# Two-layer decoder trunk: block norm's sum by two float32r products, stacked gate weights, 640 keys in two halves, sooner split of transposed probabilities in layer 1

## The chip, the cores and the metric

One core of a Trainium2 chip runs the whole program. The metric is the time of one execution in device microseconds (us); with one core, the slowest core is that core. TensorE (PE) multiplies, VectorE (DVE) and ScalarE (ACT) work on what it leaves in PSUM, GpSimd (POOL) helps, and SyncE (SP) issues most transfers. Each engine works its own list of instructions in order; semaphores tie the lists together.

## What is computed

Two decoder layers over 1024 positions of width 1024, in float32. Layer 0 uses differential attention (8 heads with two score maps each), layer 1 forgetting attention (16 heads with a learned decay). Each is followed by a residual with layer norm, a gated MLP of width 2816 with a causal convolution, and another layer norm. Cut to what the change touches:

```python
# layer 0, per block of 128 queries
s = einsum('bhcqd,bhckd->bhcqk', qb, k) * scale
p = masked_softmax(s, causal_mask(start, Q_BLOCK, S))
a = p[:, :, 0] - lam * p[:, :, 1]
o = einsum('bhqk,bhkd->bqhd', a, v)
o = rms_norm(o, subln_g) * (1.0 - lambda_init)   # mean of squares over the 128 of a head
# layer 1
q, k, v, f_logit = split(x @ w_in, ...)          # f_logit: 16 columns
log_f = log_sigmoid(f_logit + b_f); c = cumsum(log_f, axis=1)
s = einsum('bhqd,bhkd->bhqk', qb, k) * scale + cb[..., :, None] - c[..., None, :]
o = einsum('bhqk,bhkd->bqhd', masked_softmax(s, mask), v)
```

## The kernel before

**Number form.** A float32 operand x is split into a high part (x rounded to float32r, by an ACT copy, L89) and a low part (the rest, by a DVE subtraction, L91 or L93). A product of two split operands is three float32r products, high by high, high by low and low by high: `mm3`, L100 to L102. The low by low product is left out everywhere. Where one operand is a transposed probability of layer 1, two products do (L1397 and L1398).

**Attention by pairs.** `attention(l)` goes over 8 pairs of 64-wide head parts. During a pair its scores, softmax and value products run, and in between the projections of the next pair (`project`, 48 steps) are fed to PE as filler; in the last pair the filler is the output projection. A job is one block of 128 queries of one score map. Its parts are spread over ticks: `scores` (L533, L534), the mask and row minimum on DVE (`top`, L540) with the first tick; the exponential on ACT (L578, layer 1 L694) and the division on DVE (L581 to L588, layer 1 L697 and L698) later. A block of query number qt has (qt+1) x 128 keys, and `scores` takes them in chunks of up to 512 columns, so 640 keys are a chunk of 512 and one of 128. Each chunk has two products.

**Values.** When the blocks of a group (four query blocks; in the last pair of layer 0 also two groups of two) are done, a `Values` object turns their probabilities with PE transposes (`turn_one`, L1371) into a PSUM tile "m", splits them (`evacuate`, tiles "pt" from the pool probT with three buffers) and multiplies them with the values (`products`). One round of the main loop is `tick` (next job's scores, products of what is split, `evacuate`, exponentials, divisions), some projection steps, and `tock` (`turn`, `finish`), with the remaining steps behind. So transposes of one tock are split in the next tick and multiplied in the one after. The pool for "m" has four banks, shared by projections, transposes, values and sums.

**Block norm.** In layer 0, `diff_values` ends a group: ACT copies the values to "of" (L600) and squares them (L602); one float32 product with a 128 x 128 tile of ones (L606) sums over the head; ACT takes the logarithm and the exponential (L608, L609), and four DVE operations (L610 to L613) apply the result.

**Gate logits.** At the start of layer 1, `gate_logits(c)` multiplies the 16 gate columns with the 8 blocks of x, three products each, for the two halves c of the positions; DVE adds the bias (L636). The first call stands at the seam of layer 0's MLP and layer 1, the second inside `first_pair`.

**What sets the order.** The Python code gives a program order; a scheduler then orders the instructions of every engine by its own picture of what is ready, and the buffer pools decide the waits. So an edit in one place can move instructions elsewhere. Weights come by transfer into "wst" tiles (two buffers, used in layer 0 for probabilities too) and are cut into "wh" and "wl" by ACT and DVE.

## Time and profile before

| quantity | value |
|---|---|
| median of 3 runs (lowest to highest) | 2470.56 us (2469.18 to 2472.64) |
| profiled execution, its own time | 2472.59 us |
| its span, first to last instruction | 2470.8 us |
| PE busy in the span | 2421.0 us, 11377 matmul records |
| DVE, ACT, POOL busy | 1893.9, 1239.2, 141.2 us |
| mean granted clock of TensorE | 0.994 |
| layer 0's attention from 98 to 435 us: PE, DVE, ACT busy | 329.60, 266.99, 189.76 us of 337 |
| layer 1's attention from 1280 to 1740 us: PE, DVE, ACT busy | 456.96, 354.50, 257.83 us of 460 |

A row of the timeline has the start in us from the span's start, the duration in us, engine, line, operation, output and inputs by the program's names (buffer numbers left out), the shape, the count, and in brackets the idle time before it and what ended it. PE records overlap: the next matmul starts before the last one's listed end. A row of the windows has the stretch, its length, then busy time and count for PE, PEld (weight loads), DVE, ACT and POOL, the granted clock, the share of the DMA engines and GB/s.

### The profile page before, as it was taken

The page shows a single profiled execution, that of the slowest core. Times are in us where ns is not written, and L with a number is a line of the kernel's source. Part 1 is how long each engine was busy: PE and PEld are TensorE (multiplying, and loading weights), DVE is VectorE, ACT ScalarE, POOL GpSimd, SP SyncE. Part 2 cuts the span into 40 slices and gives each one's busy share as a digit, 9 for nine tenths or more (in the row PEclk, how much of TensorE's full clock was granted, in tenths as well). Part 3 has the DMA queues.
Part 4 walks back from the last instruction along what each step waited for, and adds up shares of the span by engine and source line. Part 5 has one row for each costly group of instructions (what it writes and reads, how often), then busy time and mean ns, then how long its engine had stood idle before and what let it go on. Part 6 is the DMA issues. An engine that isn't in the chain of part 4 may idle for free. (4 is left out here: it accounts for less than half of the span.)

```text
span 2470.8 us, 32550 instructions
## 1 busy us (share of the span) xinstructions
PE 2421.0 (98%) x11377; PEld 1984.9 (80%) x11377; DVE 1893.9 (77%) x3588; ACT 1239.2 (50%) x2311; POOL 141.2 (6%) x323
## 2 busy tenths in 40 slices
PE   9999999999999999989999999999999999999998
PEld 7887778778888888878778888888878888888776
DVE  5887877989767667696857777778888666666978
ACT  4555556556544444434545555555465444445344
POOL 2111111010000000000100000000010000000000
PEclk9999999999999999999999999999999999999999
DMA  6223223532322224842422222224223222228622
GB/s 182 65 84 91 81 82 92 174 110 80 103 77 77 95 85 140 298 157 74 138 70 73 65 65 65 65 81 155 94 79 101 77 89 90 77 85 301 206 86 98
DMA packets 111940, 266.02 MB, mean 108 GB/s; under 512 B 17648, under 2 KB 24816, under 8 KB 111776
## 3 DMA queue, kind: packets, MB, share of 16 engines
q1 hardware_dynamic: 110816, 262.83, 33.4%
q8 instruction: 90, 1.47, 0.2%
q0 software_dynamic: 672, 1.05, 0.2%
q14 instruction: 74, 0.61, 0.1%
q10 hardware_dynamic: 288, 0.07, 0.0%
HBM read 182.68 MB, written 47.64 MB: 93 GB/s over the span
## 5 line engine op out<-in xcount | busy, mean ns | idle before, releaser
L100 PE MATMUL m<-xh,wh 128*128 128x512 f32 x768 | 320.3, 417 | 7.0 <-DVE pt L91 6.6
L101 PE MATMUL m<-xl,wh 128*128 128x512 f32 x768 | 302.7, 394 | 1.7 <-DVE xl L91 1.7
L102 PE MATMUL m<-xh,wl 128*128 128x512 f32 x768 | 302.8, 395 | 0.0
L100 PE MATMUL m<-xh,wo 128*128 128x512 f32 x656 | 255.4, 389 | 0.0
L102 PE MATMUL m<-xh,wo 128*128 128x512 f32 x656 | 255.3, 389 | 0.0
L101 PE MATMUL m<-xl,wo 128*128 128x512 f32 x656 | 255.2, 389 | 0.0
L89 ACT ACTIVATE pt<-m 128x512 fp32r<-128x512 f32 (+3 forms) x285 | 137.6, 492 | 182.8 <-PE m L1371 120.6
L540 DVE CUSTOM_DVE_ANT_0 s<-s,mask 128x384 f32<-128x384 f32 (+7 forms) x256 | 194.5, 760 | 42.4 <-PE s L534 41.5
L89 ACT ACTIVATE wo<-wg 128x512 fp32r<-128x512 f32 x168 | 106.5, 634 | 225.0 <-PE m L102 218.4
L100 PE MATMUL m<-q,wo 128*128 128x512 f32 x472 | 184.1, 390 | 0.0
L91 DVE TENSOR_TENSOR pt<-m,pt 128x512 fp32r<-128x512 f32 (+3 forms) x285 | 156.7, 558 | 35.6 <-ACT pt L89 31.7
L101 PE MATMUL m<-q,wo 128*128 128x512 f32 x472 | 183.8, 389 | 0.0
L102 PE MATMUL m<-q,wo 128*128 128x512 f32 x472 | 183.7, 389 | 0.0
L100 PEld LDWEIGHTS m<-xh,wh 128*128 128x128 f32 x768 | 145.7, 190 | 38.3 <-DVE pt L91 11.2
L102 PEld LDWEIGHTS m<-xh,wl 128*128 128x128 f32 x768 | 145.0, 189 | 31.3 <-DVE wl L91 0.2
L101 PEld LDWEIGHTS m<-xl,wh 128*128 128x128 f32 x768 | 145.5, 190 | 27.5 <-issue 2.9
L89 ACT ACTIVATE wo<-t 128x512 fp32r<-128x512 f32 x132 | 82.8, 627 | 145.3 <-PE m L102 133.2
L91 DVE TENSOR_TENSOR wo<-wg,wo 128x512 fp32r<-128x512 f32 x168 | 115.3, 687 | 41.1 <-ACT wo L89 40.2
L527 POOL CAST qz<-q 64x128 fp32r<-64x128 f32 x256 | 96.6, 378 | 845.1 <-PE s L534 773.2
L100 PEld LDWEIGHTS m<-xh,wo 128*128 128x128 f32 x656 | 123.1, 188 | 26.0 <-ACT pt L1093 0.6
L101 PEld LDWEIGHTS m<-xl,wo 128*128 128x128 f32 x656 | 123.1, 188 | 25.7
L102 PEld LDWEIGHTS m<-xh,wo 128*128 128x128 f32 x656 | 123.1, 188 | 25.6 <-DVE wo L91 0.2
(341 smaller groups left out, 5875.6 us busy)
## 6 DMA issues: line engine op xcount, KB each, us to landing
wst<-in_w SPq DMA_DIRECT2D x46, 512.0 KB, 3.9
t<-in_wi SPq DMA_DIRECT2D x44, 512.0 KB, 4.5
ad<-t SPq DMA_DIRECT2D x44, 512.0 KB, 3.7
ha<-ad SPq DMA_DIRECT2D x88, 256.0 KB, 5.5
wg<-in_wi SPq DMA_DIRECT2D x42, 512.0 KB, 3.5
wb<-in_wd SPq DMA_DIRECT2D x84, 256.0 KB, 3.2
q<-q SPq DMA_DIRECT2D x128, 128.0 KB, 2.2
pt<-in_wd SPq DMA_DIRECT2D x48, 256.0 KB, 4.5
```

The costliest lines, as they stand in the source:

```text
L89: nc.scalar.activation(hi, src, AF.Copy, scale=1.0 if scale is None else scale)
L91: nc.vector.tensor_tensor(lo, src, hi.bitcast(F32), op=ALU.subtract)
L100: mm(out, wh, xh, start=start, stop=False)
L101: mm(out, wh, xl, start=False, stop=False)
L102: mm(out, wl, xh, start=False, stop=stop)
L527: nc.gpsimd.tensor_copy(qz[r:r + 64, :], q[r:r + 64, qt * P:qt * P + P])
L540: self.nc.vector.tensor_tensor_reduce(sb[:, :ln], sb[:, :ln], self.mask[:, 1024 - ln:], 1.0, BIG, ALU.add, ALU.min, mn)
```

## The change

Five edits.

1. *Block norm.* For pairs 0 to 6 the squares are split, and the sum is two float32r products by ones (high and low part). The last pair keeps the float32 product. The reciprocal root goes to a tile of its own ("rd", from the pool bcast; in the last pair a "pt" tile), ACT squares it, and three DVE operations instead of four apply it.
2. *Gate logits.* The high and low parts of the gate weights stand side by side in one tile of 48 columns per block (16 high, 16 zeros, 16 low), taken from the "pt" buffers instead of a tile of its own. One product by the high part of x gives both sums, in rows 0 to 15 and 32 to 47; a second one takes the high weights by the low part of x. DVE adds rows 32 to 47 in an operation of its own. POOL writes the zeros.
3. *640 keys.* Two chunks of 320, set so that they meet at the border of the two PSUM banks.
4. *Layer 1's splits.* `evacuate` runs in `tock`, right behind the transposes, and no longer in the next `tick`. In layer 0 it stays.
5. *The tile of ones* is float32r, read as float32 where it was read as such.

```diff
@@ -134,8 +134,8 @@
             for t in self.qz[h]:
                 nc.gpsimd.memset(t[64 - 64 * h:128 - 64 * h, :].bitcast(F32), 0.0)
         self.nz = [0, 0]
-        self.ones = cp.tile([P, P], F32, name="ones")
-        nc.vector.memset(self.ones, 1.0)
+        self.ones = cp.tile([P, P], F32R, name="ones")
+        nc.vector.memset(self.ones.bitcast(F32), 1.0)
         self.cw, self.cb = [], []
         for l in range(2):
             cw = cp.tile([P, NF, 3], F32, name=f"cw{l}")
@@ -528,8 +528,10 @@
         m = 66 if l else P
         ln = (qt + 1) * P
         sb = self.sbank()
-        for c in range((ln + 511) // 512):
-            ks = slice(c * 512, min(ln, c * 512 + 512))
+        w = ln // 2 if ln == 640 else 512
+        sb = sb[:, 512 - w:512 - w + ln]
+        for c in range(0, ln, w):
+            ks = slice(c, min(ln, c + w))
             nc.tensor.matmul(sb[:, ks], q[:, qt * P:qt * P + P], kd[:, ks], start=True, stop=False)
             nc.tensor.matmul(sb[:, ks], qz[:m], kl[:m, ks], start=False, stop=True)
         return sb, ln
@@ -594,22 +596,32 @@
             self.ofs[p] = self.otile()
         return self.ofs[p]
 
-    def diff_values(self, of, ob, q0, q1):
+    def diff_values(self, of, ob, q0, q1, p):
         nc, w = self.nc, (q1 - q0) * P
         osl = of[:, q0 * P:q1 * P]
         nc.scalar.copy(osl, ob[:, :w])
-        rd = self.tp.tile([P, 512], F32, tag="sq", name=self.nm("sq"), bufs=1)[:, :w]
-        nc.scalar.activation(rd, osl, AF.Square)
+        sq = self.tp.tile([P, 512], F32, tag="sq", name=self.nm("sq"), bufs=1)[:, :w]
+        nc.scalar.activation(sq, osl, AF.Square)
+        last = p == NP - 1
+        if not last:
+            hl = self.lp.tile([P, 1024], F32R, tag="lg", name=self.nm("hl"))
+            h, l = hl[:, :w], hl[:, 512:512 + w]
+            self.split(h, l, sq)
         for _ in range(1 + FL):
             yield
         ms = self.mbank()[:, :w]
-        nc.tensor.matmul(ms, self.ones, rd, start=True, stop=True)
-
+        if last:
+            nc.tensor.matmul(ms, self.ones.bitcast(F32), sq, start=True, stop=True)
+            rd = self.tt.tile([P, 1024], F32, tag="pt", name=self.nm("rd"))[:, :w]
+        else:
+            nc.tensor.matmul(ms, self.ones, h, start=True, stop=False)
+            nc.tensor.matmul(ms, self.ones, l, start=False, stop=True)
+            rd = self.lp.tile([P, 1024], F32, tag="lg", name=self.nm("rd"))[:, :w]
         nc.scalar.activation(rd, ms, AF.Ln, scale=1.0 / P, bias=self.eps_rms)
         nc.scalar.activation(rd, rd, AF.Exp, scale=-0.5)
-        nc.vector.scalar_tensor_tensor(ms, ms, P * RMS_EPS, rd, op0=ALU.add, op1=ALU.mult)
+        nc.scalar.activation(sq, rd, AF.Square)
         nc.vector.scalar_tensor_tensor(osl, osl, self.gsub, rd, op0=ALU.mult, op1=ALU.mult)
-        nc.vector.tensor_tensor(ms, ms, rd, op=ALU.mult)
+        nc.vector.scalar_tensor_tensor(ms, ms, P * RMS_EPS, sq, op0=ALU.add, op1=ALU.mult)
         nc.vector.scalar_tensor_tensor(osl, ms, -3.0 * P, osl, op0=ALU.add, op1=ALU.mult)
 
     def otile(self):
@@ -620,8 +632,9 @@
         if c == 0:
             st = self.tmp()[:, :P]
             nc.sync.dma_start(st, self.i["wf"])
-            self.wf = [self.cp.tile([P, 128], F32R, name=f"wf{j}") for j in range(2)]
-            self.split(*self.wf, st)
+            self.wf = self.tt.tile([P, 1024], F32R, tag="pt", name="wf")[:, :48 * KT].rearrange("p (k n) -> p k n", k=KT)
+            nc.gpsimd.memset(self.wf[:, :, 16:32].bitcast(F32), 0.0)
+            self.split(self.wf[:, :, :16], self.wf[:, :, 32:], st.rearrange("p (k n) -> p k n", k=KT))
             self.bf = self.cp.tile([16, 1], F32, name="bf")
             nc.sync.dma_start(self.bf, self.i["bf"])
             self.z = self.tmp()
@@ -630,10 +643,13 @@
             nc.sync.dma_start(self.tri, self.i["tri"])
         ps = self.mbank()
         for kt in range(KT):
-            ws = slice(16 * kt, 16 * kt + 16)
-            self.mm3(ps[:16], self.wf[0][:, ws], self.wf[1][:, ws], self.xh[kt, c], self.xl[kt, c],
-                     kt == 0, kt == KT - 1)
-        nc.vector.tensor_scalar(self.z[:16, c * 512:c * 512 + 512], ps[:16], self.bf, None, op0=ALU.add)
+            both = self.wf[:, kt], self.xh[kt, c]
+            high = self.wf[:, kt, :16], self.xl[kt, c]
+            for i, (w, x) in enumerate((both, high) if kt == 0 else (high, both)):
+                nc.tensor.matmul(ps[:w.shape[1]], w, x, start=kt + i == 0, stop=kt == KT - 1 and i == 1)
+        z = self.z[:16, c * 512:c * 512 + 512]
+        nc.vector.tensor_scalar(z, ps[:16], self.bf, None, op0=ALU.add)
+        nc.vector.tensor_tensor(z, ps[32:48], z, op=ALU.add)
 
     def forget_gates(self):
 
@@ -655,7 +671,7 @@
             nc.vector.scalar_tensor_tensor(l, l, 1.0 / k, u if k > 1 else e, op0=ALU.add, op1=ALU.mult)
         nc.vector.tensor_scalar(z, z, 0.0, None, op0=ALU.min)
         nc.vector.scalar_tensor_tensor(l, l, -2.0, z, op0=ALU.mult, op1=ALU.add)
-        nc.vector.tensor_tensor_scan(c, self.ones, l, 0.0, op0=ALU.mult, op1=ALU.add)
+        nc.vector.tensor_tensor_scan(c, self.ones.bitcast(F32), l, 0.0, op0=ALU.mult, op1=ALU.add)
         self.c, self.cw8 = c, w
 
     def forget_sums(self):
@@ -784,7 +800,8 @@
         for v in values:
             v.products()
         for v in values:
-            v.evacuate()
+            if v.l == 0:
+                v.evacuate()
         keep = []
         for e in live:
             e[1] += 1
@@ -808,6 +825,9 @@
         n = 1 if values and values[0].l == 0 else 2
         for v in values:
             n -= v.turn(n)
+        for v in values:
+            if v.l:
+                v.evacuate()
         for v in values:
             v.finish()
         return [v for v in values if not v.over]
@@ -1398,7 +1418,7 @@
                     mm(o, self.v[0][:, vs], l, start=False, stop=last)
                 if last:
                     a = k.of_tile(self.p), self.ob, self.q0, self.q1
-                    self.end = k.diff_values(*a) if self.l == 0 else k.fox_values(*a, self.h)
+                    self.end = k.diff_values(*a, self.p) if self.l == 0 else k.fox_values(*a, self.h)
                     self.ob = None
         self.hl = []
 
```

The scheduler then makes another order in many places. Three of them follow, as the built programs have it.

ACT in layer 0, around the border of two pairs, before. L89 is the copy of a split ("pt" transposed probabilities, "q" queries and keys, "wh" a weight cut out of "wst"), L578 an exponential, L608 and L609 the norm, L458 a projection's result:

```order
L89 ACTIVATE pt_2104<-m_2073 128x256
L578 ACTIVATE wst_2110,ls_2059<-s_2052,nm_2057 128x768
L89 ACTIVATE q_1676<-t_1703 128x512
L89 ACTIVATE q_1678<-t_1704 128x512
L89 ACTIVATE wh_2224<-wst_2142 128x1024
L608 ACTIVATE sq_2028<-m_2114,eps_rms 128x512
L89 ACTIVATE pt_2161<-m_2112 128x128
L609 ACTIVATE sq_2028<-sq_2028 128x512
L578 ACTIVATE p_2168,ls_2100<-s_2093,nm_2098 128x896
L458 ACTIVATE t_1704<-m_2039 128x512
L578 ACTIVATE wst_2213,ls_2157<-s_2150,nm_2155 128x896
```

The same place now (L580 the exponential, L620 to L622 the norm with its new Square):

```order
L89 ACTIVATE pt_2122<-m_2091 128x256
L580 ACTIVATE wst_2128,ls_2077<-s_2070,nm_2075 128x768
L89 ACTIVATE q_1689<-t_1718 128x512
L89 ACTIVATE q_1691<-t_1719 128x512
L89 ACTIVATE pt_2181<-m_2130 128x128
L620 ACTIVATE rd_2135<-m_2132,eps_rms 128x512
L580 ACTIVATE p_2188,ls_2118<-s_2111,nm_2116 128x896
L621 ACTIVATE rd_2135<-rd_2135 128x512
L458 ACTIVATE t_1719<-m_2057 128x512
L622 ACTIVATE sq_2043<-rd_2135 128x512
L89 ACTIVATE wh_2247<-wst_2162 128x1024
L580 ACTIVATE wst_2233,ls_2177<-s_2170,nm_2175 128x896
```

The last split of the group, "pt" of 128 columns, stood behind the weight cut "wh" and the first step of the norm; now it stands ahead of both, and so do the norm and two more operations. On DVE the subtraction of that split has moved ahead of "wl" in the same way, at the end of pairs 0 to 5, but not of pair 6.

DVE at the seam to layer 1, behind the first gate call, before. L1476 to L1510 are layer norm, "wl" the low parts of the first two weights of layer 1, L636 the bias of the gate logits:

```order
L1476 TENSOR_SCALAR nm_11097<-sums_9401 128x1
L91 TENSOR_TENSOR wl_11178<-wst_11175,wh_11177 128x1024
L91 TENSOR_TENSOR wl_11184<-wst_11181,wh_11183 128x1024
L1487 TENSOR_SCALAR n_2033_11098<-n_2033_11098 128x1
L1510 SCALAR_TENSOR_TENSOR p_9353<-p_9353,nm_11097,lg_9402 128x768
L1489 SCALAR_TENSOR_TENSOR n_2035_11100<-n_2034_11099,n_2033_11098 128x1
L636 TENSOR_SCALAR t_11136<-m_11140,bf 16x512
```

The same place now (L651 the bias, L652 the added rows 32 to 47):

```order
L1496 TENSOR_SCALAR nm_11170<-sums_9474 128x1
L651 TENSOR_SCALAR t_11209<-m_11213,bf 16x512
L91 TENSOR_TENSOR wl_11244<-wst_11241,wh_11243 128x1024
L1507 TENSOR_SCALAR n_2064_11171<-n_2064_11171 128x1
L1530 SCALAR_TENSOR_TENSOR p_9426<-p_9426,nm_11170,lg_9475 128x768
L1509 SCALAR_TENSOR_TENSOR n_2066_11173<-n_2065_11172,n_2064_11171 128x1
L652 TENSOR_TENSOR t_11209<-m_11213,t_11209 16x512
L1513 SCALAR_TENSOR_TENSOR n_2065_11172<-n_2066_11173,n_2065_11172 128x1
L91 TENSOR_TENSOR wl_11250<-wst_11247,wh_11249 128x1024
```

The bias, which reads the gate's sum, has moved from behind both cuts to ahead of the first.

PE in layer 1, in the middle of a pair, before. L1371 is a transpose into a PSUM tile "m", L1397 and L1398 are the value products by the high and low part of a split "pt"; pt_14136 and pt_14139 are the splits of transposes some 35 rows earlier, and the split of the tile m_14152 transposed here is first multiplied some 30 rows later:

```order
L1371 MATMUL m_14152<-ident,t_14009 128x128
L1371 MATMUL m_14152<-ident,p_14067 128x128
L102 MATMUL m_14077<-xh_11015,wl_13967 128x512
L100 MATMUL m_14077<-xh_11059,wh_13966 128x512
L101 MATMUL m_14077<-xl_11060,wh_13966 128x512
L102 MATMUL m_14077<-xh_11059,wl_13967 128x512
L533 MATMUL s_14172<-q_13380,q_13378 128x512
L534 MATMUL s_14172<-q_13382,qz_281 128x512
L1397 MATMUL m_14178<-pt_14136,q_12723 128x512
L1398 MATMUL m_14178<-pt_14136,q_12723 128x512
L1397 MATMUL m_14178<-pt_14139,q_12723 128x512
L1398 MATMUL m_14178<-pt_14139,q_12723 128x512
```

The corresponding place now (L1391 the transpose, L1417 and L1418 the value products, L535 and L536 the scores); pt_14225 is the split of the tile m_14217 that is transposed here:

```order
L1391 MATMUL m_14217<-ident,p_13971 128x128
L1391 MATMUL m_14217<-ident,p_14015 128x128
L1391 MATMUL m_14217<-ident,t_14072 128x128
L1391 MATMUL m_14217<-ident,p_14130 128x128
L102 MATMUL m_14146<-xh_11132,wl_14037 128x512
L535 MATMUL s_14243<-q_13449,q_13447 128x512
L536 MATMUL s_14243<-q_13451,qz_281 128x512
L1417 MATMUL m_14202<-pt_14222,q_12792 128x512
L1418 MATMUL m_14202<-pt_14222,q_12792 128x512
L1417 MATMUL m_14202<-pt_14225,q_12792 128x512
L1391 MATMUL m_14258<-ident,p_13971 128x128
L1418 MATMUL m_14202<-pt_14225,q_12792 128x512
```

From the last transpose to the first product by its split there are five products of PE, with a transpose for the next tile before the product by the low part.

## The prediction

> **What bounds the kernel now.** I read the page first, then TensorE's waits, then the groups by shape, and last the timeline of PE, DVE, ACT at each place that the diff touches. The page settles which engine counts.
>
> ```profile
> PE 2421.0 (98%) x11377; PEld 1984.9 (80%) x11377; DVE 1893.9 (77%) x3588; ACT 1239.2 (50%) x2311; POOL 141.2 (6%) x323
> ```
>
> TensorE is busy for 98% of the span, in every stage. So a product that goes is worth its time on PE, and work that goes to ACT or DVE is free unless PE comes to wait for it. What PE waits for now (engine line, us in total, times, longest):
>
> ```profile
> PE m L100 <- DVE pt L91: 7.1, 7, 1.7
> PE s L100 <- DVE acc L1267: 6.5, 3, 3.3
> PE m L963 <- POOL acc L1512: 4.0, 2, 2.1
> PE m L503 <- DVE of L613: 1.4, 1, 1.4
> PE m L1371 <- DVE q L91: 1.1, 6, 0.2
> ```
>
> The largest entry is a projection product that waits for a PSUM bank ("m") which DVE frees when it has split transposed probabilities ("pt"). The next two are in the MLP and its layer norm, which the diff doesn't touch.
>
> A matmul's listed duration overlaps the next one's, so its price is the distance of starts. Thirty products of 512 columns in a row after the first gate call run from here to here:
>
> ```profile
> 1219.23 0.39 PE L100 MATMUL m<-xh,wh 128*128 128x512 f32 x1
> 1225.84 0.39 PE L102 MATMUL m<-xh,wl 128*128 128x512 f32 x1
> ```
>
> That is 6.61 us over 29 distances: 0.228 us per float32r product of 512 columns.
>
> The Trainium skill, "TensorE: Matmul & The Clock Gate", section "Back-to-back issue gap", gives about 131 ns as the sustained distance at 512 columns; by it the sixteen gate products removed below would be 2.1 us instead of 3.65. The trace disagrees (0.228 us), and the measured price is used.
>
> **Part 1: the norm's sum.** The float32 product by ones in the middle of a run:
>
> ```profile
> 186.41 1.02 PE L606 MATMUL m<-sq,ones 128*128 128x512 f32 x2
> 186.87 0.80 PE L100 MATMUL m<-xh,wh 128*128 128x512 f32 x1
> 187.50 0.39 PE L101 MATMUL m<-xl,wh 128*128 128x512 f32 x1
> ```
>
> One such product is two records, and it also delays the product behind it: from its start to that of L101 it is 1.09 us, which holds one L100 of 0.228, so it costs 0.86. Two float32r products cost 0.456. Saved 0.406, for 14 of the 17 sums (pairs 0 to 6, two groups each; pair 7 keeps float32): **5.7 us**.
>
> Beside PE: each of the 14 groups gains a copy on ACT and a subtraction on DVE (the split), every group gains a Square on ACT, and one of DVE's four closing operations goes. The nearest rows, and the load of that stage:
>
> ```profile
> 190.31 0.63 ACT L609 ACTIVATE sq<-sq 128x512 f32<-128x512 f32 x1
> 192.31 0.70 DVE L612 TENSOR_TENSOR m<-m,sq 128x512 f32<-128x512 f32 x1
> 98.00:435.00 337.00, 329.60 (x1632) 268.56 (x1631) 266.99 (x630) 189.76 (x397) 41.38 (x94) 1.00 0.29 83
> ```
>
> ACT gets 31 x 0.63 = 20 us more over the whole attention of layer 0; in 337 us of it ACT is busy for 190, so there is room. DVE gets 14 operations and loses 17, about nothing. What stands in the way of PE is when they come, not how many; that is part 4. The bank of the sum is freed one DVE operation sooner. I cost this side at nothing, within one 0.70 either way per pair where the cover fails. Pair 7's result in a "pt" tile has the same bound, in one pair.
>
> **Part 2: 640 keys as 320 + 320.** The scores of one row block of 640 keys and what follows:
>
> ```profile
> 1343.33 0.39 PE L533 MATMUL s<-q,q 128*128 128x512 f32 x1
> 1343.56 0.40 PE L534 MATMUL s<-q,qz 66*128 66x512 f32 x1
> 1343.80 0.23 PE L533 MATMUL s<-q,q 128*128 128x128 f32 x1
> 1343.86 0.27 PE L534 MATMUL s<-q,qz 66*128 66x128 f32 x1
> 1343.97 0.33 PE L1397 MATMUL m<-pt,q 128*128 128x256 f32 x1
> 1344.14 0.28 PE L1398 MATMUL m<-pt,q 128*128 128x256 f32 x1
> 1303.64 0.28 PE L533 MATMUL s<-q,q 128*128 128x256 f32 x1
> 1303.76 0.28 PE L534 MATMUL s<-kl,qz 66*128 66x256 f32 x1
> 1303.88 0.39 PE L1371 MATMUL m<-ident,p 128*128 128x128 f32 x2
> ```
>
> The second 128-column product takes 0.11, and the 256-column one behind it 0.17, where undisturbed 256-column products (last three rows) take 0.12. A short product leaves no time to load the next weights. So the block costs 0.81 less that 0.12, 0.69. A product of 320 columns isn't in the trace; between 256 (0.12) and 512 (0.228) on a line it is 0.147, four make 0.59. Saved 0.10, in 8 pairs x 2 x 2 layers = 32 blocks: **3.3 us**. Bounds: at four times 0.14 it is 4.2, at four times 0.175, nearer to 384 columns, nothing. I take the line, since it lies between two measured shapes. The mask pass and the exponential read the same 640 columns at another offset: nothing.
>
> **Part 3: gate logits.** Three products per block and half become two: 8 x 2 = 16 fewer, 16 x 0.228 = 3.65 us, half of it in each call. Behind the first call, though, DVE decides:
>
> ```profile
> 1217.76 0.20 DVE L1476 TENSOR_SCALAR nm<-sums 128x1 f32<-128x1 f32 x1
> 1217.89 1.63 DVE L91 TENSOR_TENSOR wl<-wst,wh 128x1024 fp32r<-128x1024 f32 x1
> 1222.66 0.73 DVE L636 TENSOR_SCALAR t<-m,bf 16x512 f32<-16x512 f32 x1
> 1218.99 0.40 PE L102 MATMUL m<-xh,wf 128*16 128x512 f32 x1
> 1219.70 0.40 PE L102 MATMUL m<-xh,wl 128*128 128x512 f32 x1
> ```
>
> DVE's cut "wl" ends about 1219.5, just ahead of the first product that reads it (1219.70). In the new order the bias addition (0.73) stands before that cut, and waits for the gate sum. PE ends the gate 1.82 sooner, at about 1217.4, runs four projection products that need no wl, and is at 1218.3; DVE starts the bias at 1217.9, ends it at 1218.6 and the cut at 1220.2. In the old kernel the same product with the same four before it would start at 1219.70 + 0.46 = 1220.16. The first call's 1.82 is thus lost again: stall gone, wl late instead. The second call has no such neighbour. **1.8 us**, with bounds 0 and 3.65. The zero rows, the wider result and the second addition over 16 rows lie beside other work; the weights now borrow a "pt" tile, which no split needs before the first values of layer 1.
>
> **Part 4: the order in layer 0.** The wait of 7.1 us, seen at one pair's boundary:
>
> ```profile
> 188.61 1.06 ACT L89 ACTIVATE wh<-wst 128x1024 fp32r<-128x1024 f32 x1 [2.01 <-DMA wst<-in_w]
> 190.15 0.27 ACT L89 ACTIVATE pt<-m 128x128 fp32r<-128x128 f32 x1
> 189.71 1.23 DVE L91 TENSOR_TENSOR wl<-wst,wh 128x1024 fp32r<-128x1024 f32 x1 [1.25 <-ACT wh L89]
> 190.85 0.28 DVE L91 TENSOR_TENSOR pt<-m,pt 128x128 fp32r<-128x128 f32 x1
> 191.19 0.50 PE L100 MATMUL m<-xh,wh 128*128 128x512 f32 x1 [1.68 <-DVE pt L91]
> ```
>
> ACT stands 2.01 us at the weight cut for its transfer; behind it in both queues is the last split of 128 columns, and PE waits for the bank that this split frees. The new order puts that split ahead of the cut, on ACT and on DVE, at six of the pair boundaries (the order piece on ACT shows one). Then ACT's split needs only its transposes, which stand in PE's queue ahead of the sum's product at 186.41, and PE's bank is free before it is asked for. What is late next is the cut, some 2 us later on DVE; but its weights are first multiplied behind the next group's sum, far later. Of the 7.1 I take **5.5**, some 0.9 at each of six boundaries; bounds 0 (another wait takes the place) and 7.1.
>
> **Part 5: layer 1 splits sooner.** In the stage of layer 1 PE waits hardly at all:
>
> ```profile
> 1280.00:1740.00 460.00, 456.96 (x2397) 377.95 (x2396) 354.50 (x804) 257.83 (x557) 38.39 (x119) 1.00 0.28 82
> ```
>
> At most 3 us are to be had in 460. The split now comes in the tick of its transposes and the products one tick earlier, so PE has less other work between transpose and product. The chain in between is:
>
> ```profile
> 1390.59 0.60 ACT L89 ACTIVATE pt<-m 128x512 fp32r<-128x512 f32 x1
> 1390.94 0.49 DVE L698 TENSOR_SCALAR p<-p,rs 128x512 f32<-128x512 f32 x1
> 1391.34 0.68 DVE L91 TENSOR_TENSOR pt<-m,pt 128x512 fp32r<-128x512 f32 x1
> ```
>
> Copy and subtraction 1.28, with one multiplication ahead on DVE 1.77. At the narrowest place of a pair (the order piece on PE) PE has one projection product, two score products, two value products, one high value product and one transpose, 6 x 0.228 + 0.11 = 1.48, before it needs the low part. So it waits for 0 to 0.29 there, 2.3 us in eight pairs, against up to 3 us of bank waits that the sooner split may end. I take **0**, bounds -3 and +2.3.
>
> **Sum.** 5.7 + 3.3 + 1.8 + 5.5 + 0 = 16.3 us. The profiled execution took 2472.59 us (span 2470.8), so it would be 2456.3; it lies 2.0 above the median of the runs, 2470.56, and the forecast for the median is 2454.3.
>
> **The clock.** PE's granted clock falls for one slot after the wait of L503:
>
> ```profile
> 441.13 0.44 PE L503 MATMUL m<-ident,t 128*128 128x128 f32 x2 [1.41 <-DVE of L613]
> 439.41:442.82 3.41, 1.62 (x11) 0.93 (x9) 3.41 (x11) 1.02 (x3) 0.41 (x1) 1.00 0.96 335
> 442.82:446.23 3.41, 3.41 (x8) 2.70 (x9) 2.43 (x5) 0.19 (x1) 0.00 (x0) 0.50 1.03 339
> ```
>
> A slot in which PE was busy for 1.62 of 3.41 us is followed by one at 0.50, which costs 1.7 us. The Trainium skill, "TensorE: Matmul & The Clock Gate", section "Why this matters for your kernels", asks only for no idle gaps over about 3 us; by it shorter waits never cost clock, and nothing changes here. The trace disagrees: no gap in that slot was over 1.8. By the trace one slot more or less is possible, 1.7 either way; it is in the range, not in the sum.
>
> **Rivals.** *Better still* (0.15): layer 1's waits go (2), two reduced slots go (3.4) and the first gate call keeps its gain (1.8): 7.2 more, 2447.1. For it: all three are PE waits on DVE, which is relieved at those places. Against: each needs its own luck.
>
> *Given back in layer 0* (0.12): the split and the Square put 1.26 us more on ACT per group; if PE meets that at each of seven boundaries (8.8) and the 5.5 doesn't come, 2.0 remains, 2468.5. For it: at these boundaries ACT and DVE are both late now. Against: ACT there stood idle for 2.01.
>
> *Slower* (0.07): the short handover of layer 1 makes PE wait at every tick with transposes, 12 a pair, 96 in all. At the 0.29 of the narrowest place it is 28 us, 2482.1. It decides from 0.22 a tick, (16.3 + 4.9) / 96. For it: DVE is busy for 354 of 460 us there, so the subtraction may queue. Against: elsewhere in the pair PE has more work between. That the split sum runs as slowly as before (no 5.7: 2460.0) is held unlikely and lies in the range: every float32r row costs one pass.
>
> **How the numbers follow.** The forecast has 0.66, by its own bounds 2449 to 2461. The range 2446 to 2466 takes in most of the better case and the edge of the given-back one. A measurement tells about 0.2%, 4.9 us, from no change: faster is below 2465.6, slower above 2475.5. Faster: 0.66 + 0.15 + 0.01; same: 0.11; slower: 0.07.
>
> **What would show it.** Right: L606 only three times and pairs of products by hl in its place, 0.23 apart; 320-column scores 0.15 apart; "PE m L100 <- DVE pt L91" nearly gone; a wait of L102 for wl behind the first gate call. Wrong: a new wait of L1417 or L1418 for pt in layer 1 of several us in total, PE waits in layer 0 as long as before under another name, or a result above 2466.

## The result and the profile after

The changed kernel takes 2453.24 us (median of 4 runs, 2452.17 to 2458.73) against 2469.87 us for the kernel before in the same measurement (4 runs, 2466.36 to 2472.64). The ratio is 0.9937, 95% interval 0.9922 to 0.9952: faster by 16.6 us, where 16.3 was forecast. The profiled execution took 2452.95 us, its span is 2451.2. By the spans of the two profiled executions, 2470.8 and 2451.2, the difference is 19.6. The total is right, but its terms are not; two large errors of opposite sign lie under it, and the profile shows both.

Busy times and instructions on the page of the kernel after:

```profile
PE 2405.2 (98%) x11361; PEld 1983.5 (81%) x11361; DVE 1891.5 (77%) x3587; ACT 1248.4 (51%) x2342; POOL 143.0 (6%) x324
```

TensorE is still the engine that counts; it lost 15.8 us of busy time. Its waits, from the list of who waited for whom:

```profile
PE m L983 <- POOL acc L1532: 4.9, 3, 2.4
...
PE m L503 <- ACT t L458: 2.5, 4, 1.2
PE s L535 <- DMA q<-q: 1.6, 1, 1.6
...
PE m L102 <- DVE n L1507: 1.3, 1, 1.3
```

The entry of 7.1 us, L100 for DVE's "pt", has fallen to 0.7 and no longer leads the list. Two waits are new in it, L535 for a transfer "q" and L102 behind the gates, and L503's wait for ACT's "t" grew from 0.7 to 2.5.

**The norm's sum.** Before (first fence, the transpose ahead of the sum; its other rows stand in the prediction) and after, starts and durations on PE:

```profile
186.30 0.27 PE L1371 MATMUL m<-ident,p 128*128 128x128 f32 x1
```

```profile
182.76 0.27 PE L1391 MATMUL m<-ident,p 128*128 128x128 f32 x1
182.78 0.48 PE L617 MATMUL m<-hl,ones 128*128 128x512 f32 x1
183.10 0.40 PE L618 MATMUL m<-hl,ones 128*128 128x512 f32 x1
...
183.56 0.40 PE L101 MATMUL m<-xl,wh 128*128 128x512 f32 x1
```

From the transpose to L101 it was 187.50 - 186.30 = 1.20 us and is 183.56 - 182.76 = 0.80. So one sum saves 0.40, the other thirteen save 0.39 to 0.44 by the same rows, and 14 save 5.6.

**The order at a pair's border.** ACT, after:

```profile
184.21 0.26 ACT L89 ACTIVATE pt<-m 128x128 fp32r<-128x128 f32 x1
187.44 1.07 ACT L89 ACTIVATE wh<-wst 128x1024 fp32r<-128x1024 f32 x1
```

The split of 128 columns now stands 3.2 us ahead of the weight cut, and the cut, coming later, finds its transfer done. PE's waits in the stretch from 98 to 404 us, which holds five borders, before and after:

```profile
PE m L100 <- DVE pt L91: 5.5, 5, 1.7
PE m L1371 <- DVE of L613: 0.7, 1, 0.7
```

```profile
PE m L1391 <- DVE of L625: 1.2, 5, 0.3
PE m L503 <- ACT t L458: 0.5, 2, 0.3
```

6.2 us became 1.7: 4.5 at five borders, the 0.9 each that was forecast.

**640 keys.** PE after, the four score products of one block and what follows:

```profile
1329.71 0.30 PE L535 MATMUL s<-q,q 128*128 128x320 f32 x1
1329.85 0.32 PE L536 MATMUL s<-q,qz 66*128 66x320 f32 x1
1330.00 0.33 PE L535 MATMUL s<-q,q 128*128 128x320 f32 x1
1330.16 0.32 PE L536 MATMUL s<-q,qz 66*128 66x320 f32 x1
1330.32 0.40 PE L100 MATMUL m<-xh,wh 128*128 128x512 f32 x1
```

0.61 us for four, 0.153 each (0.147 was interpolated). The old block cost 0.69, so 0.08 is saved, in 32 blocks 2.6 us.

**The gates.** First and last gate product, before and after:

```profile
1209.80 0.48 PE L100 MATMUL m<-xh,wf 128*16 128x512 f32 x1
1247.01 0.40 PE L102 MATMUL m<-xh,wf 128*16 128x512 f32 x1
```

```profile
1196.84 0.47 PE L649 MATMUL m<-xh,wf 128*48 128x512 f32 x1
1204.20 0.39 PE L649 MATMUL m<-xh,wf 128*48 128x512 f32 x1
1206.82 0.50 PE L102 MATMUL m<-xh,wl 128*128 128x512 f32 x1 [1.30 <-DVE n L1507]
1226.83 0.50 PE L535 MATMUL s<-q,q 128*128 128x128 f32 x2 [1.63 <-DMA q<-q]
1233.27 0.40 PE L649 MATMUL m<-xh,wf 128*48 128x512 f32 x1
```

The stretch was 37.21 us and is 36.43. The sixteen products are gone (3.65), but two new waits take 2.9 of it back: L102, which reads "wl", and the first score product for the transfer of its operands. (The row names "n" for L102; on DVE the cut "wl" ends at 1206.76, just ahead of the product.)

**Layer 1's attention.** The first transpose behind it, before and after:

```profile
1794.12 0.49 PE L963 MATMUL m<-ident,acc 128*128 128x128 f32 x3
```

```profile
1774.90 0.49 PE L983 MATMUL m<-ident,acc 128*128 128x128 f32 x3
```

From the last gate product to here it was 547.11 us and is 541.63: 5.5 less, of which the shorter scores are 1.3 (16 x 0.08). The transposes of probabilities inside it, groups by shape from 1250 to 1735 us, before and after (count, busy us, mean ns, idle before them):

```profile
L1371 PE MATMUL m<-ident,p 128*128 128x128 f32 x344 | 68.6, 278 | 2.8 <-DVE q L91 1.1 <-DVE pt L91 0.3 <-DVE acc L849 0.2
```

```profile
L1391 PE MATMUL m<-ident,p 128*128 128x128 f32 x353 | 66.6, 273 | 0.0
```

Their 2.8 us of idle time are gone, many short waits for PSUM banks. Some were too short for the list of waits, which had eight here, of 0.2 or 0.3 us and 1.6 in all.

**The last pair of layer 0.** The 12th sum of 17, and the first transpose behind layer 0's attention, before and after:

```profile
415.02 1.02 PE L606 MATMUL m<-sq,ones 128*128 128x512 f32 x2
544.18 0.49 PE L963 MATMUL m<-ident,acc 128*128 128x128 f32 x3
```

```profile
402.46 0.48 PE L617 MATMUL m<-hl,ones 128*128 128x512 f32 x1
533.75 0.38 PE L983 MATMUL m<-ident,acc 128*128 128x128 f32 x2
```

Up to the 12th sum 12.6 us were gained (1.7 of them by a slot at half clock that only the kernel before has there, at 94.7 us), but the stretch between these rows grew from 129.16 to 131.29, although three sums at 0.40 and two blocks at 0.08 should have cut it by 1.4. So 3.5 us are lost there, and layer 0 ends 10.4 ahead. The largest of PE's waits in the last pair, before (415 to 545 us) and after (415 to 535):

```profile
PE m L100 <- DVE pt L91: 1.6, 2, 1.1
PE m L503 <- DVE of L613: 1.4, 1, 1.4
PE m L100 <- DVE acc L849: 0.6, 1, 0.6
PE m L100 <- DVE rs L581: 0.4, 1, 0.4
```

```profile
PE m L100 <- DVE rs L583: 1.5, 2, 1.1
PE m L503 <- ACT t L458: 1.2, 1, 1.2
PE m L100 <- DVE acc L869: 1.2, 1, 1.2
PE m L503 <- DVE acc L869: 1.0, 1, 1.0
PE m L100 <- DVE pt L91: 0.5, 1, 0.5
```

The wait for "pt" fell here too, by 1.1, and that for the norm's "of" is gone. In their place the list has longer waits, put down to "rs" (the reciprocal row sums of a softmax), "t" (a projection's result) and "acc" (the addition of residual rows on DVE). Within the stretch the listed waits add up to 4.5 us before and 6.4 after, so the list has 1.9 of the 3.5.

Two stretches with no changed instruction, the feed-forward parts, came out 2.5 and 0.4 us shorter. Over the fourteen profiles of this study the first took 662.3 to 668.6 us, longer or shorter without regard to the edit and with none to three slots at half clock in it; single profiles carry that much chance.

### The profile page after: what moved, and what is told of

It reads as the page before. It is cut to its first block, busy times and chain, and to the rows that moved or that the text cites. A ratio compares the mean times of both kernels' runs of the same rounds, so it can differ in the third digit from the quotient of the medians.

```text
span 2451.2 us, 32545 instructions
## 1 busy us (share of the span) xinstructions
PE 2405.2 (98%) x11361; PEld 1983.5 (81%) x11361; DVE 1891.5 (77%) x3587; ACT 1248.4 (51%) x2342; POOL 143.0 (6%) x324
## 5 line engine op out<-in xcount | busy, mean ns | idle before, releaser
L100 PE MATMUL m<-xh,wh 128*128 128x512 f32 x768 | 314.3, 409 | 0.5 <-ACT xh L89 0.3
L102 PE MATMUL m<-xh,wl 128*128 128x512 f32 x768 | 303.1, 395 | 1.3 <-DVE n L1507 1.3
L101 PE MATMUL m<-xl,wh 128*128 128x512 f32 x768 | 301.7, 393 | 1.5 <-DVE xl L91 1.5
L100 PE MATMUL m<-xh,wo 128*128 128x512 f32 x656 | 255.3, 389 | 0.0
L102 PE MATMUL m<-xh,wo 128*128 128x512 f32 x656 | 255.2, 389 | 0.0
L101 PE MATMUL m<-xl,wo 128*128 128x512 f32 x656 | 255.2, 389 | 0.0
L89 ACT ACTIVATE wo<-wg 128x512 fp32r<-128x512 f32 x168 | 106.3, 633 | 229.6 <-PE m L102 218.6
L89 ACT ACTIVATE pt<-m 128x512 fp32r<-128x512 f32 (+3 forms) x285 | 131.3, 491 | 116.9 <-PE m L1391 113.0
L100 PE MATMUL m<-q,wo 128*128 128x512 f32 x472 | 184.1, 390 | 0.0
L101 PE MATMUL m<-q,wo 128*128 128x512 f32 x472 | 183.8, 389 | 0.0
L102 PE MATMUL m<-q,wo 128*128 128x512 f32 x472 | 183.7, 389 | 0.0
L102 PEld LDWEIGHTS m<-xh,wl 128*128 128x128 f32 x768 | 144.7, 188 | 32.8 <-DVE wl L91 1.7
L100 PEld LDWEIGHTS m<-xh,wh 128*128 128x128 f32 x768 | 145.0, 189 | 27.0 <-DVE pt L91 2.4
L101 PEld LDWEIGHTS m<-xl,wh 128*128 128x128 f32 x768 | 145.4, 189 | 25.4 <-DVE xl L91 1.8
L89 ACT ACTIVATE wo<-t 128x512 fp32r<-128x512 f32 x132 | 82.7, 626 | 145.2 <-PE m L102 133.3
L100 PEld LDWEIGHTS m<-xh,wo 128*128 128x128 f32 x656 | 123.1, 188 | 25.8 <-ACT pt L1113 0.3
L101 PEld LDWEIGHTS m<-xl,wo 128*128 128x128 f32 x656 | 123.1, 188 | 25.6
L102 PEld LDWEIGHTS m<-xh,wo 128*128 128x128 f32 x656 | 123.1, 188 | 25.6
```

The costliest lines, as they stand in the source:

```text
L89: nc.scalar.activation(hi, src, AF.Copy, scale=1.0 if scale is None else scale)
L100: mm(out, wh, xh, start=start, stop=False)
L101: mm(out, wh, xl, start=False, stop=False)
L102: mm(out, wl, xh, start=False, stop=stop)
```

## The experiments

All ratios are to the kernel before, with 95% intervals.

**Theories.** A: the terms of the prediction add, each part is worth its TensorE price plus the waits that its order ends. B: waits only move, so that a part alone is worth something else than within the whole. For the end of layer 0 a third question came up: what takes 3.5 us back.

**Each part alone** on the kernel before. Run 1, the norm's sum with its new closing and order:

```diff
-        nc.tensor.matmul(ms, self.ones, rd, start=True, stop=True)
+            nc.tensor.matmul(ms, self.ones, h, start=True, stop=False)
+            nc.tensor.matmul(ms, self.ones, l, start=False, stop=True)
```

> The kernel before with the block norm's edit alone (split squares, two float32r products, three closing operations; the last pair in float32). My theory, that the parts add up: 14 sums at 0.41 less on PE give 5.7 us, and the moved split at six pair borders gives 5.5 to 6.4 more, so 11 to 12 us below the kernel before, with the wait of L100 for DVE pt (7.1 before) near nothing in the profile. Rival, that the order's gain needs the other edits or is luck: the wait stays at some 7 us and only 5.7 us go.

Measured: 2463.22 us, ratio 0.9986 (0.9977 to 0.9996): 3.5 us by the ratio, 4.5 by the medians, where 11 to 12 were expected. The 12th sum came 11.4 us sooner. The two terms promise 9 up to there (eleven sums, five borders), and two slots at half clock, 3.4 us, stand ahead of it in the kernel before and none in this profile. The end of layer 0 came only 5.5 us sooner; the stretch between grew to 135.04, with one slot more in it (1.7). The gain is made and then in large part given back in the last pair.

Run 2, the halves of 320:

```diff
+        w = ln // 2 if ln == 640 else 512
+        sb = sb[:, 512 - w:512 - w + ln]
```

> The kernel before with 640 keys as two halves of 320 alone. My theory: 32 blocks at 0.10 less, 3.3 us below the kernel before, nothing else moves in the profile's waits. Rival, that a 320-column product costs as much as one of 384 (0.175): no gain.

Measured: 2463.28, ratio 0.9982 (0.9973 to 0.9991), 4.5 us with an interval from 2.2 to 6.7. The rows give 2.6, and 3.3 were expected.

Run 3, the gates:

```diff
-            self.mm3(ps[:16], self.wf[0][:, ws], self.wf[1][:, ws], self.xh[kt, c], self.xl[kt, c],
+            for i, (w, x) in enumerate((both, high) if kt == 0 else (high, both)):
```

> The kernel before with the stacked gate weights alone. My theory: 16 products fewer, 3.65 us on PE, of which the first call's half is lost to a wait of L102 for the cut wl of 1.3 to 2.0 us behind the first call; 1.8 us below the kernel before. Rival, that nothing waits: 3.65 us below and no wait of L102 there.

Measured: 2467.10, ratio 0.9996 (0.9987 to 1.0005). The gates alone can't be told from nothing; the rows give 0.8. The wait of L102 came as expected (1.3 us), and the score product's wait for its transfer, which was not expected, stands in this profile too (1.6).

Run 4, layer 1's sooner split:

```diff
-            v.evacuate()
+            if v.l == 0:
+                v.evacuate()
...
+            if v.l:
+                v.evacuate()
```

> The kernel before with layer 1's split in the tick of its transposes alone. My theory in the prediction: nothing to be had, within -3 and +2.3 us. Rival, which the changed kernel's profile suggests (from the first to the last score of layer 1 it gained 4.2 us, of which the 640 keys explain 1.6): 2 to 3 us below the kernel before, from PE's waits for PSUM banks at the transposes, those of under 0.2 us included. Rival on the other side: products wait for their split at many ticks, and it is slower.

Measured: 2462.15, ratio 0.9978 (0.9969 to 0.9988), 5.4 us. This part was forecast at nothing. Layer 1's stretch took 1791.25 - 1248.95 = 542.30 us in place of 547.11, 4.8 less without shorter scores:

```profile
1248.95 0.40 PE L102 MATMUL m<-xh,wf 128*16 128x512 f32 x1
1791.25 0.49 PE L967 MATMUL m<-ident,acc 128*128 128x128 f32 x3
```

The four ratios of the parts multiply to 0.9942; the whole is 0.9937. Theory A holds for the total, as far as intervals of 0.0009 to either side of each part can tell. It doesn't hold for the parts: 3.5, 4.4, 1.0 and 5.4 us, where 11.2, 3.3, 1.8 and 0 were forecast.

**Order without price** (run 5): the kernel after with the float32 product, the cut of the squares left in place and unused.

```diff
-            nc.tensor.matmul(ms, self.ones, h, start=True, stop=False)
-            nc.tensor.matmul(ms, self.ones, l, start=False, stop=True)
+            nc.tensor.matmul(ms, self.ones.bitcast(F32), sq, start=True, stop=True)
```

> The changed kernel with the float32 product by ones put back in all pairs, while the squares are still split (the split's results are then not used). This parts the order from the price on PE. My theory, that both count by themselves: 14 x 0.41 = 5.7 us slower than the changed kernel, and the wait of L100 for DVE pt stays near nothing. Rival, that the shorter sum is what frees the border of the pairs: 10 us or more slower, with that wait back at about 7 us.

Measured: 2460.57, ratio 0.9973 (0.9965 to 0.9982), by the ratios 8.9 us behind the whole change. At the 12th sum it stood 6.0 ahead of the kernel before, 6.6 behind the kernel after; eleven sums at 0.40 are 4.4 of that. VectorE's order shifts a little with the dearer product (at a border the cut "wl" stands ahead of the norm's operations again, not behind them), and L503 waits 2.9 us for ACT's "t" in the stretch from 98 to 404 us where after has 0.5. The wait of L100 for "pt" does not come back in that stretch, so it isn't the shorter sum that frees the border. Price and order both count. The 6.0 also hold a clock slot of 1.7 that only the kernel before has at 94.7 us.

**The late "wl"** (run 6): the first gate call's two bias operations are written behind the first projection's result.

```diff
+                if c == 0 and s == 0:
+                    self.gate_bias(0)
...
+        self.gps = ps
+
+    def gate_bias(self, c):
```

> The changed kernel with the two additions of the first gate call written behind the first projection's result, so that on DVE they stand behind both cuts wl again. My theory: the wait of L102 behind the first gate call (1.30 us in the profile) goes, and the changed kernel becomes 1.3 to 1.8 us faster. Rival, that another wait takes its place at the seam: no difference.

Measured: 2454.28, ratio 0.9947 (0.9932 to 0.9961), no gain. PE, and DVE ahead of it:

```profile
1207.61 0.50 PE L102 MATMUL m<-xh,wl 128*128 128x512 f32 x1 [1.07 <-DVE wl L91]
```

```profile
1204.87 1.00 DVE L1542 SCALAR_TENSOR_TENSOR acc<-acc,n,lg 128x768 f32<-128x768 f32 x1
1205.92 3.31 DVE L91 TENSOR_TENSOR wl<-wst,wh 128x1024 fp32r<-128x1024 f32 x2
```

The wait is 1.07 in place of 1.30 with no bias ahead of the cut. What stands there is the layer norm's work ("acc", 1.00 us), and the cut follows it without a gap on DVE. Counted from the first gate product (1197.84 here) the cut starts 8.08 us behind it, in the kernel after 8.72: 0.64 sooner. But it takes 1.65 us (3.31 for two), in the kernel after 1.20, and so it ends only 0.2 sooner. The bias is about half of the wait; why the cut takes longer without it no run shows.

**The closing alone** (run 7): on the kernel before, a Square on ACT as the closing's third operation there, three operations on DVE, the root in a tile of its own; one float32 product and no cut. That tile is one of the three "pt" buffers in every pair, while the kernel after takes "pt" in the last pair alone and a "bcast" tile in the other seven.

```diff
+        nc.scalar.activation(sq, rd, AF.Square)
-        nc.vector.tensor_tensor(ms, ms, rd, op=ALU.mult)
```

> The kernel before with the closing of three DVE operations and ACT's Square alone: no split, float32 product in all pairs, order at the pair borders as before. My theory, that DVE's operation is beside PE: no difference to the kernel before (within 1.5 us), and the wait of L100 for DVE pt stays at about 7 us. Rival, that the sooner freed bank of the sum is what helped: 5 us or more below the kernel before.

Measured: 2472.88, ratio 1.0022 (1.0013 to 1.0032): 5.4 us slower. From the waits of PE from 98 to 404 us, and PE at the last sum:

```profile
PE m L1381 <- DVE of L623: 2.6, 5, 1.2
```

```profile
530.61 0.70 PE L612 MATMUL m<-sq,ones 128*128 128x256 f32 x2 [0.91 <-ACT sq L602]
```

In the old order the closing comes later by ACT's third operation, and a transpose waits for the bank of the sum: 2.6 us where before had 0.7. These 1.9 and the 0.9 at the last sum are half of the 5.4; what the rest is, and whether the "pt" tile has a part in it, no run shows. Is there such a price in the kernel after too? Run 9 asks.

**Without the sooner split** (run 8), the rest of the change kept:

```diff
-            if v.l == 0:
-                v.evacuate()
+            v.evacuate()
...
-            if v.l:
-                v.evacuate()
```

> The kernel after with the transposed probabilities of layer 1 split where the kernel before splits them. If the 4.2 us that layer 1's attention gained in the kernel after are the sooner split's (the run with that part alone gained 3.5 us there and 1.3 us behind it), this kernel loses 3 to 5 us there: about 2457 (2456 to 2458.5). If they are the shorter scores and the shifted order's, as the prediction's nothing for this part has it, it stands at the kernel after's 2453 within 1.5 us, and the stretch from the second gate product to the last product with the keys stays within 1 us of the kernel after's.

Measured: 2460.41, ratio 0.9966 (0.9955 to 0.9976), by the ratios 7.2 us behind the whole. The stretch of layer 1 and its transposes:

```profile
1236.17 0.39 PE L649 MATMUL m<-xh,wf 128*48 128x512 f32 x1
1782.26 0.49 PE L979 MATMUL m<-ident,acc 128*128 128x128 f32 x3
```

```profile
L1387 PE MATMUL m<-ident,p 128*128 128x128 f32 x351 | 70.1, 278 | 2.8 <-DVE q L91 1.1 <-DVE pt L91 0.3 <-DVE acc L865 0.2
```

546.09 us, against 541.63; the idle 2.8 us are back, with the same releasers. So the sooner split is worth 4.5 us in these rows with it taken out, and 4.8 with it put in alone. The other profiles agree: this stretch took 545.9 to 547.1 us in all six without the sooner split and 540.7 to 542.3 in all eight with it, each with and without the halves of 320, and no slot at half clock falls into any of them. The distances of starts from one transpose to the next, 502 or 501 in the stretch, add up to 60.0 to 60.1 us in the six and to 55.6 to 55.7 in the eight: some 4.4 us, the size of the gain. What is left of the 7.2 lies outside: the first feed-forward part took 666.16 us here and 663.08 in the kernel after, with one slot more.

**What takes the last pair's gain** (runs 9 to 12; the stretch from the 12th sum is 131.29 us in the kernel after, with one slot at half clock in it). Layer 0 is the same in runs 6 and 8, where the stretch took 131.08 and 134.31, with one slot and two. Without the slots these three are 129.6, 129.4 and 130.9, so a microsecond or so in this stretch is chance. Run 9, the old closing in every pair:

```diff
-        nc.scalar.activation(sq, rd, AF.Square)
+        nc.vector.tensor_tensor(ms, ms, rd, op=ALU.mult)
```

> The kernel after with the closing of the kernel before in every pair: the reciprocal root is taken in the tile of the squares, no third Square on ScalarE, four operations on VectorE; the cut of the squares and the two float32r products stay. The closing alone made the kernel before 5.4 us slower. If that price adds to the other parts, this kernel is about 5 us faster than the kernel after: near 2448 (2446 to 2450). If the price was of the order that only the float32 product leaves (both closing operations behind the weight cuts), or of the profile's clock slots, it is within 2 us of 2453; VectorE then has 0.68 us more work in each of 16 sums, so 2453 to 2456.

Measured: 2452.67, ratio 0.9935 (0.9923 to 0.9948); the stretch 130.30, also with one slot. In the kernel after the new closing has no price that these times could tell, and at most 1.0 of the 3.5 us is its own, as much as chance. So the price of run 7 belongs to what differs there, the old order or the "pt" tile in every pair; no run parts these two. Theory B holds for this part.

Run 10, the old closing in the last pair alone:

```diff
+            rd = sq
-            rd = self.tt.tile([P, 1024], F32, tag="pt", name=self.nm("rd"))[:, :w]
```

> The kernel after with only the last pair closed as in the kernel before (root in the tile of the squares, four operations on VectorE, no probability tile held). If the last pair's 4 us between the 12th sum and the end of layer 0 go to the probability tile that the closing holds there, this is 2 to 4 us faster than the kernel after: about 2450, and the stretch of 131.3 us falls to 127 to 129. If they go to the order at the border before it, or to VectorE's full queue, nothing changes: 2453 within 1.5 us, the stretch 131 to 132.

Measured: 2453.57, ratio 0.9938 (0.9926 to 0.9951); the stretch 130.40, with no slot in it. The tile held by the closing isn't it.

Run 11, the old order at the last border alone:

```diff
-        last = p == NP - 1
+        last = p >= NP - 2
```

> The kernel after with the squares of the seventh pair (of eight) left uncut and its sum one float32 product, like the last pair's: at the last border the closing then stands behind the weight cuts, as in the kernel before; the six borders ahead keep the order of the kernel after. If the moved order costs the last pair its 4 us, this one loses 0.8 us by two dearer products and gains 3 to 4: about 2450.5 (2449.5 to 2451.5), the stretch from the 12th sum to the end of layer 0 at 128 to 129.5 us in place of 131.3. If the last pair is held by something the order there does not set, it is 0.5 to 1.5 us slower than the kernel after: 2454, the stretch at 132.

Measured: 2459.24, ratio 0.9960 (0.9945 to 0.9975): not faster than the kernel after, and 5.7 us slower by the ratios, whose intervals still touch.

The stretch (from 403.79 to 533.47) is 129.68, 1.6 shorter with 0.8 of dearer products in it, but no clock slot at 0.50 falls into it, and one (1.7 us) does in the kernel after. Without that slot the kernel after would have 129.6: what the old order gains, 0.7 or so, goes to the dearer products. The wait for residual rows is gone here, on DVE and on PE, but L503 waits 1.4 us for the norm's "of" again. What is lost in the profiled execution lies in the first feed-forward part (668.15 us against 663.08), which the edit doesn't touch, and in eight stretches at 0.50 against six.

Run 12, VectorE's subtractions for the output projection in that stretch on GpSimd (they turned out to be fourteen):

```diff
-            self.split(self.oh[k, c], self.ol[k, c], src[:, c * 512:c * 512 + 512])
+                self.nc.gpsimd.tensor_tensor(self.ol[k, c], x, self.oh[k, c].bitcast(F32), op=ALU.subtract)
```

> The kernel after with 13 of VectorE's subtractions around the last pair of layer 0 (the low halves of the block outputs that the output projection reads, 0.60 to 0.69 us each, some 8 us in all) made by GpSimd instead; the six borders ahead keep their order. GpSimd's 128x256 operation takes 0.74 us, so 1.5 us are expected for 128x512, an estimate. If VectorE's full queue is what takes back 4 us in the last pair (46 of its 53 us there are busy), the stretch from the 12th sum to the end of layer 0 falls from 131.3 to 127 to 129 and the total to about 2450 (2449 to 2452). If the last pair is held by the chain through ScalarE and the transfers, the stretch stays at 130 to 132 and the total at 2453; if GpSimd comes too late with a half, a wait of TensorE for it shows and the stretch grows to 133 to 137.

Measured: 2458.86, ratio 0.9961 (0.9947 to 0.9976): slower than the kernel after, with intervals that touch. The stretch goes from 401.96 to 536.31. In 53 us of it (415 to 468) DVE is busy for 42.02 us, in the kernel after for 45.92. DVE at a transfer, in this run and in the kernel after:

```profile
463.15 1.29 DVE L874 SCALAR_TENSOR_TENSOR acc<-acc,m 128x512 f32<-128x512 f32 x2 [2.18 <-DMA acc<-in_x]
```

```profile
462.94 1.29 DVE L869 SCALAR_TENSOR_TENSOR acc<-acc,m 128x512 f32<-128x512 f32 x2 [1.51 <-DMA acc<-in_x]
```

DVE is busy for 3.9 us less and the stretch grows to 134.35: less work on DVE didn't bring the gain back. That DVE's load has no part in the loss isn't shown by this, since GpSimd takes about twice as long for a half, 1.29 to 1.39 us. The stretch is the one expected for halves that come too late, but TensorE waits only 0.6 us for them by name, and 4.5 for the residual addition L874 on DVE. One piece shows in both runs: DVE waits for the transfer of residual rows, 2.18 and 1.51 us, where the kernel before waited 0.75:

```profile
474.06 1.28 DVE L849 SCALAR_TENSOR_TENSOR acc<-acc,m 128x512 f32<-128x512 f32 x2 [0.75 <-DMA acc<-in_x]
```

That is 0.8 of the 3.5 on DVE; PE's own waits for this addition are 0.6, 2.2 and 4.5 us in the kernel before, the kernel after and run 12. The rest stays open: it is not the tile that the closing holds, at most 1.0 is the closing, taking work off DVE alone didn't help, and the order at the border ahead of it could not be shown to be it.

## Why the prediction was right, step by step

| step | forecast, us | measured, us |
|---|---|---|
| two products for the sum | 5.7 | 5.6 (14 x 0.40) |
| 640 keys | 3.3 | 2.6 (32 x 0.08) |
| gates | 1.8 | 0.8 |
| order at six borders | 5.5 | 4.5 at five; at the sixth the wait for "pt" fell by 1.1, inside the next row |
| the last pair of layer 0, sixth border included | not in the sum | -3.5 |
| layer 1's sooner split | 0 | 4.5 (4.8 alone) |
| a clock slot | range only | 1.7 (one at 94.7 us is gone) |
| sum | 16.3 | 16.2; by medians 16.6 |

The two profiles differ by 19.6 us; 2.9 of these lie in the two stretches with no changed instruction and 0.5 in no row of the table.

**Part 1** is right to 0.1. Its cost beside TensorE, "nothing", held in the kernel after (run 9), yet not everywhere: run 7 has 5.4 us for the closing in the old order, with its root in a "pt" tile.

**Part 2**: right in kind, 0.02 a block too much.

**Part 3**: the wait of L102 for "wl" came, 1.30 us for the 1.82 named. The reason given, the bias ahead of the cut, is about half of it: without the bias the cut starts 0.64 sooner, but takes 0.45 longer (run 6). What failed is "The second call has no such neighbour": ahead of the second call the first score product waits 1.63 us for the transfer of its operands. A transfer of "ql" close to it took 4.9 us from issue to landing where the kernel before had 3.7, and a weight's 512 KB now go out between the two of "ql", not ahead of them; whether that is the reason no run shows.

**Part 4**: right at five borders, which held 5.5 of the 7.1 us. The step that failed is the sixth: "some 0.9 at each of six boundaries" took the last border for one like the others. Behind it the output projection runs, which loads its own operands and residual rows, and there more than its gain is given back. The rival that put a give-back at every border, by ACT's added work, was wrong about the place: the five borders gave all that they were to give.

**Part 5** is the term that was mis-sized: "I take 0", and it is 4.5. Two steps failed. "At most 3 us are to be had in 460" was read from the listed idle time, 2.8 us at the transposes; by the distance of starts 4.5 were to be had there (run 8). That a matmul's modelled end covers part of the wait ahead of the next is a likely reason, not a shown one. And the loss set against it, "2.3 us in eight pairs" at the narrowest place, didn't come: the only wait of a value product for "pt" on the list of this stretch is one of 0.4 us (L1417). The slower rival, which needed 0.22 us at each of 96 ticks, falls with it.

That the forecast is within 1.1 us of the median is chance in part: 4.5 and 1.7 too little against 0.1, 0.7, 1.0, 1.0 and 3.5 too much.

## What to carry to other kernels

Read a row of short waits by the distance of starts, not by the idle time that is listed: 2.8 us of it stood beside 4.5 to be had. When a wait is removed at every border of a loop, look at the last border by itself; what follows it is other work with its own transfers. And price an edit in the kernel that it will run in: the closing cost 5.4 us alone in the old kernel, and taking it out of the new one gained nothing.

## What the runs showed of the hardware

A float32r product of 320 columns starts 0.153 us before the next. On GpSimd the subtraction of 128x512 took 1.29 to 1.39 us (18.9 us for fourteen), on VectorE two of them 1.28 to 1.38 in the same place of the kernel after.

TensorE's clock falls to 0.50 three to eight times in a profile, for one slot of 3.41 us or two (6.83), and the last time at the program's end. The number differs between the profiles: seven in that of before, six in after, three in run 2, eight in run 11. At 1.7 us a slot this can be a large part of what single runs differ by. Two neighbouring slots of the kernel after:

```profile
425.87:429.28 3.41, 1.88 (x11) 1.13 (x10) 3.41 (x9) 1.67 (x6) 0.29 (x1) 1.00 0.81 238
429.28:432.69 3.41, 3.20 (x8) 2.55 (x9) 2.38 (x7) 0.47 (x1) 0.00 (x0) 0.50 0.91 240
```

Again it follows a slot in which PE was busy for about half (1.88 of 3.41), here by waits of 0.37 and 0.99 us. The Trainium skill, "TensorE: Matmul & The Clock Gate", section "Why this matters for your kernels", names idle gaps over about 3 us; the trace disagrees once more, with 0.99 as the longest here. No threshold comes out of these figures: in the same profile the slots from 535.1 and 1224.6 us, with PE busy for 1.61 and 1.78, are followed by none at 0.50. The slot at 94.7 us in the kernel before, or one at 96, stands in the profiles of runs 2, 4 and 7, which leave the squares whole, and in none that cuts them; run 3 leaves them whole too and has none there, so the link isn't shown.
